# Which queue asks for a small on-chip copy: the doubling of the keys' high part, moved from ScalarE's queue to SP's

## The chip, the cores and the metric

The kernel runs on one core of a Trainium2 chip. A core has a matrix engine (PE, with its weight loads shown as PEld), a vector engine (VectorE, DVE in the profile), a scalar engine (ScalarE, ACT), a general engine (GpSimd, POOL) and SyncE (SP), which here only asks for transfers. The transfers themselves are carried out by 16 DMA engines; any engine's queue can ask for one, and two queues do in this kernel, SP's and ScalarE's. The metric is the device time of one execution in microseconds, the median of several runs.

## The reference

One layer of a hybrid decoder on 1024 tokens of width 1024, in float32:

```python
u = rms_norm(x, norm1_g)
aq, ak, av, hq, hf, hi, hg = jnp.split(u @ w_in, IN_SPLITS, axis=-1)
attn = rms_norm(dilated_attention(aq, ak, av), attn_norm_g)   # 8 heads of 64, three dilations
rec  = rms_norm(hgrn2_mixer(hq, hf, hi, lb), hgrn_norm_g) * silu(hg)   # 4 heads of 128
h = x + concatenate([attn, rec]) @ w_out
h = h + conv_glu(rms_norm(h, norm2_g), w_up, conv_w, conv_b, w_down)
out = rms_norm(h, final_norm_g)
```

The change lies in the attention heads. For each head, queries and keys (64 wide each) are projected from the normalised input, and each query's scores are the products with the keys before it, masked to the three dilated windows.

## The kernel before

**High and low parts.** Matrix products run on numbers that are split in two: a high part, rounded to PE's format (fp32r), and a low part, the rest. A product of two such numbers is the sum of high by high, high by low and low by high. For the scores the kernel saves a matmul with a trick of the partitions. A head is 64 wide and PE has 128 rows, so the tile `qs` holds the queries' high part in partitions 0 to 63 and their low part in partitions 64 to 127. The tile `kh` holds the keys' high part twice, in partitions 0 to 63 and again in 64 to 127: one matmul (L590) of `qs` and `kh` then gives high by high plus low by high. The second one (L591) adds the queries' high part by the keys' low part, from the tile `kl`.

**Who makes these tiles.** The function `qk_half(h, hf)` (L541) projects one head's queries and keys for one half of the tokens (512 of them), and its `evac` takes the result out of PSUM. VectorE multiplies it with the norm's factor into `x` (L550). ScalarE writes the queries' high part (L551) and the keys' high part into the upper partitions of `kh` (L552). The lower partitions are filled by another step: for heads 0 and 1 ScalarE copies from `x` once more (L554), for heads 2 to 7 a transfer copies the upper half of `kh` to its lower half (L556), 64 partitions of 512 numbers, 128 KB. VectorE then subtracts for the low parts (L557, L559). There are six heads and two halves, so L556 runs twelve times.

**The order of the work.** PE's instructions run in the order in which the code writes them (`manual_schedule` for PE alone). The instructions of the other engines and queues are ordered by the framework's planner, except where the code pins them (`keep_in_program_order`). During head h of the attention the code interleaves three kinds of work on PE: the scores of the next block of queries (`score_steps`), the transposes and value products of the present one (`value_steps`), and, as filler (`fill.run`), the projections that the next head needs. The list `beside` names that filler: `qk_block(h + 1)`, the two calls of `qk_half`, with pieces of the value projections around them. So `kh` of head h + 1 is made while head h is worked on, and the first half of its keys is read first by the scores of block 0, the second half from block 4 on.

**Scores and values.** `score_steps` multiplies, adds the mask and finds the row's extreme on VectorE (L595), takes the exponential on ScalarE (L599), and scales on POOL (L603). `value_steps` transposes the weights on PE (L618 to L625) into a PSUM tile `T` of two banks; ScalarE casts it to the high part (L628) and VectorE subtracts for the low part (L629), which also frees the bank; PE multiplies with the values (L637 to L641).

**The weights.** All weights come through the class `Ring` (L48). Its plan lists pieces of 128 by 512 numbers. For each, `fill` (L69) asks SP's queue for the load of the raw piece (L66; for the pieces of `want_iv` L253), lets ScalarE cast it to the high part (L86) and POOL or VectorE subtract for the low part (L88). There are five raw buffers and five finished pieces; `done` (L94) gives a finished piece back and calls `fill` again, so that in the code a new piece's load, cast and subtraction are written right there, inside the projection that used the old piece up. In this stage SP's queue asks for these loads alone; ahead of the stage it loads x and the mask (L391, L530), after it another mask (`hm`, L774) and later more. ScalarE's queue asks for the transfers of L556.

Of the kernel before, what the change touches and what calls it, by code (L numbers as in the profile page):

```python
# [43 lines left out]
def f32(ap):  # L44
    return ap.bitcast(F32)
# [157 lines left out]
def hybrid_kernel(ctx: ExitStack, tc: tile.TileContext, xT, w_qk, w_tok, w_hg, w_out, w_up,  # L203
                  w_down, vecs, amask, hmask, out):
    nc = tc.nc
# [245 lines left out]
    def dense(key, hf, evac, last, tag="mm"):  # L451

        t = halves[hf]
        ps = bank(tag, f"p{key}{hf}".translate({ord(x): "_" for x in "(', )"}))
        for c in range(NCT):
            hi, lo = ring.get((key, c // 4))
            s = slice((c % 4) * P, (c % 4 + 1) * P)
            b = between.get((key, hf, c), (0, 0))
            PE.matmul(ps, hi[:, s], uhi[:, c, t], start=(c == 0), stop=False)
            busy(b[0])  # L460
            PE.matmul(ps, hi[:, s], ulo[:, c, t], start=False, stop=False)
            PE.matmul(ps, lo[:, s], uhi[:, c, t], start=False, stop=(c == NCT - 1))
            busy(b[1])
            if last and c % 4 == 3:
                ring.done((key, c // 4))
            yield 0.65
        evac(ps)
# [60 lines left out]
    if True:  # L528
# [12 lines left out]
        def qk_half(h, hf, last, tag="mm"):  # L541
            t = halves[hf]

            def evac(ps):
                if hf == 0:
                    qk[h] = (at.tile([P, SEQ], F32R, tag="qs", name=f"qs{h}", bufs=NQ),
                             at.tile([P, SEQ], F32R, tag="kh", name=f"kh{h}", bufs=NQ), kls[h % NQ])
                qs, kh, kl = qk[h]
                x = at.tile([P, H2], F32, tag="x", name=f"x{h}_{hf}")
                DVE.tensor_mul(x, ps, R1[:, t])  # L550
                ACT.mul(qs[0:64, t], x[0:64], DH ** -0.5)  # L551
                ACT.copy(kh[64:128, t], x[64:128])  # L552
                if h < 2:
                    ACT.copy(kh[0:64, t], x[64:128])  # L554
                else:
                    nc.scalar.dma_start(f32(kh[0:64, t]), f32(kh[64:128, t]))  # L556
                DVE.scalar_tensor_tensor(qs[64:128, t], x[0:64], DH ** -0.5, f32(qs[0:64, t]),  # L557
                                         op0=ALU.mult, op1=ALU.subtract)
                DVE.tensor_sub(kl[0:64, t], x[64:128], f32(kh[64:128, t]))  # L559
            return dense(("qk", h), hf, evac, last, tag)  # L560
# [981 lines left out]
```

## Time and profile before

| | |
|---|---|
| median of 3 runs | 1203.69 us (1203.61 to 1204.4) |
| the profiled execution | 1204.6 us, of which 1202.6 us are the span of the trace |
| granted clock of PE | 0.997 |
| busy in the span | PE 99%, PEld 83%, DVE 79%, ACT 53%, POOL 25% |
| DMA queues | q1: 60528 packets, 101.41 MB; q10: 12176 packets, 21.44 MB |
| transfers of L556 | 12, of 128 KB each, on ScalarE's queue |
| first and last of them | 88.1 and 259.4 us from the span's start |

In the rows of the profile, a row of a group gives line, engine and operation, the tiles written and read, the count, and times; a row of the timeline gives the start and the length in microseconds, then the same, and in brackets the idle time of the engine before it with what ended it. "ACTq" and "SPq" are requests for transfers made by ScalarE's and SP's queues; they are not counted as busy time. "PE L590 MATMUL S<-kh,qs" is a score product that writes the tile S and reads `kh` and `qs`; buffer numbers are left out. In a table of stretches, each engine has its busy microseconds. Busy times of PE are partly modelled, since matmuls overlap.

### The profile page before, as it was taken

What the parts mean: (1) busy time and instruction counts of PE and PEld (TensorE: products, weight loads), DVE (VectorE), ACT (ScalarE), POOL (GpSimd) and SP (SyncE); (2) the same over time, 40 slices, a digit from 0 to 9 for tenths busy, and PEclk for the clock granted to TensorE, in tenths of its full rate; (3) what the DMA queues carried; (4) which work ended last, traced back from release to release, by engine and by line L of the source; (5) the groups of instructions that cost most, each with busy time, mean ns of one, the idle gap of its engine ahead of it and who ended that gap; (6) DMA issues with size and microseconds to landing.
All of it is one profiled execution on the core that took longest, in us unless ns stands there. A gap on an engine that the chain in (4) does not pass through costs nothing.

```text
span 1202.6 us, 17157 instructions
## 1 busy us (share of the span) xinstructions
PE 1186.7 (99%) x5854; PEld 994.9 (83%) x5854; DVE 948.9 (79%) x1776; ACT 631.5 (53%) x1219; POOL 297.9 (25%) x273
## 2 busy tenths in 40 slices
PE   9999999999999999999999999999999999999996
PEld 7988888888888888888888888888888888888886
DVE  7777776666878766485999889898888978957986
ACT  8766666667766564454543343333343444444553
POOL 1144446654001024413231222322223200000000
PEclk9999999999999999999999999999999999999998
DMA  7022222223101113432123322333223267434522
GB/s 271 13 75 62 63 62 92 80 72 115 41 31 62 61 56 115 141 129 80 44 70 114 110 83 97 123 114 120 82 97 115 96 213 251 153 101 159 169 101 89
DMA packets 72792, 123.94 MB, mean 103 GB/s; under 512 B 7552, under 2 KB 18048, under 8 KB 72704
## 3 DMA queue, kind: packets, MB, share of 16 engines
q1 hardware_dynamic: 60528, 101.41, 25.7%
q10 hardware_dynamic: 12176, 21.44, 4.9%
q8 instruction: 46, 0.75, 0.3%
q14 instruction: 42, 0.34, 0.1%
HBM read 97.65 MB, written 23.59 MB: 101 GB/s over the span
## 4 chain that ended last, share of the span: by engine, by line
PE 94%; DVE 2%; ACT 2%; issue 1%; DMA 0%; POOL 0%; SPq 0%; DVEq 0%; ACTq 0%; POOLq 0%
PE p L1143 11%; PE p L1142 11%; PE p L1141 11%; PE ds L1441 3%; PE ds L1440 3%; PE ds L1442 3%; PE po L1045 2%; PE po L1047 2%; PE po L1046 2%; PE da L1441 2%; PE da L1440 2%; PE da L1442 2%; PE S L590 1%; PE S L591 1%; PE O L637 1%; PE piv L513 1%
## 5 line engine op out<-in xcount | busy, mean ns | idle before, releaser
L88 POOL TENSOR_TENSOR wlo<-raww,whi 128x512 fp32r<-128x512 f32 x138 | 205.7, 1502 | 384.2 <-ACT whi L86 234.1
L86 ACT CAST whi<-raww 128x512 fp32r<-128x512 f32 x276 | 168.1, 617 | 191.5 <-DVE raww L120 68.6
L88 DVE TENSOR_TENSOR wlo<-raww,whi 128x512 fp32r<-128x512 f32 x139 | 99.3, 715 | 20.4 <-ACT whi L86 20.2
L86 ACT CAST whi<-r 128x512 fp32r<-128x512 f32 x70 | 43.6, 623 | 84.4 <-PE ds L1441 49.0
L603 POOL TENSOR_SCALAR P<-P,st 128x512 f32<-128x512 f32 (+2 forms) x96 | 58.0, 614 | 105.0 <-DVE st L600 90.7
L599 ACT ACTIVATE P<-P,st 128x128 f32<-128x128 f32 (+3 forms) x64 | 49.7, 777 | 26.9 <-DVE st L595 25.4
L88 DVE TENSOR_TENSOR wlo<-r,whi 128x512 fp32r<-128x512 f32 x70 | 47.9, 685 | 18.5 <-ACT whi L86 17.2
L1442 PE MATMUL ds<-fhi,wlo 128*128 128x512 f32 x160 | 62.3, 389 | 0.0
L1441 PE MATMUL ds<-flo,whi 128*128 128x512 f32 x160 | 62.3, 389 | 0.0
L1440 PE MATMUL ds<-fhi,whi 128*128 128x512 f32 x160 | 62.2, 389 | 0.0
L1141 PE MATMUL p<-b1h,whi 128*128 128x512 f32 x160 | 62.2, 389 | 0.0
L1142 PE MATMUL p<-b1l,whi 128*128 128x512 f32 x160 | 62.2, 389 | 0.0
L1143 PE MATMUL p<-b1h,wlo 128*128 128x512 f32 x160 | 62.2, 389 | 0.0
L629 DVE TENSOR_TENSOR t<-T,t 128x512 fp32r<-128x512 f32 (+1 forms) x80 | 50.7, 636 | 14.6 <-ACT t L628 13.3
L1163 DVE SCALAR_TENSOR_TENSOR cv<-g,vec,cv 128x511 f32<-128x511 f32 (+2 forms) x92 | 56.1, 614 | 4.7 <-ACT cv L1160 3.7
L628 ACT CAST t<-T 128x512 fp32r<-128x512 f32 (+1 forms) x80 | 43.1, 538 | 30.6 <-PE T L622 25.6
L1170 ACT ACTIVATE cv<-cv 128x512 f32<-128x512 f32 x44 | 27.8, 633 | 57.7 <-DVE cv L1163 57.7
L1414 POOL TENSOR_TENSOR facc<-facc,sqf 128x256 f32<-128x256 f32 x2 | 1.5, 738 | 223.4 <-ACT sqf L1413 223.4
L595 DVE CUSTOM_DVE_ANT_0 P<-S,mask 128x128 f32<-128x128 f32 (+3 forms) x64 | 35.5, 561 | 26.1 <-PE S L591 17.8
L88 DVE TENSOR_TENSOR flo<-rawf,fhi 128x512 fp32r<-128x512 f32 x70 | 47.8, 684 | 3.5 <-ACT fhi L86 3.5
L86 ACT CAST fhi<-rawf 128x512 fp32r<-128x512 f32 x70 | 43.1, 616 | 13.7 <-DMA rawf<-spT 6.6
L1440 PE MATMUL da<-fhi,whi 128*128 128x512 f32 x120 | 46.7, 389 | 0.0
(674 smaller groups left out, 3787.2 us busy)
## 6 DMA issues: line engine op xcount, KB each, us to landing
raww<-in_w_up_dram SPq DMA_DIRECT2D x88, 256.0 KB, 3.0
raww<-in_w_tok_dram SPq DMA_DIRECT2D x52, 256.0 KB, 2.7
rawf<-spT SPq DMA_DIRECT2D x40, 256.0 KB, 2.7
r<-in_w_down_dram SPq DMA_DIRECT2D x40, 256.0 KB, 3.2
raww<-in_w_hg_dram SPq DMA_DIRECT2D x32, 256.0 KB, 2.5
raww<-in_w_out_dram SPq DMA_DIRECT2D x32, 256.0 KB, 2.6
spB<-a ACTq DMA_DIRECT2D x30, 256.0 KB, 2.2
spT<-t ACTq DMA_DIRECT2D x30, 256.0 KB, 2.0
```

Source lines behind the costliest of these rows:

```text
L86: self.pin(self.high(hi[:, :w], raw))
L88: self.pin(low.tensor_sub(lo[:, :w], raw, f32(hi[:, :w])))
L599: ACT.activation(Pt[:, :n], Pt[:, :n], AF.Exp, bias=low, scale=-1.0, accum_out=st[:, 2:3])
L603: POOL.tensor_scalar(e, e, st[:, 3:4], 1.0, op0=ALU.mult, op1=ALU.mult)
L629: DVE.tensor_sub(t2[:, 1, :n], T[:, :n], f32(t2[:, 0, :n]))
L1141: PE.matmul(ps, hi[:, s], bhi, start=(start and n == 0), stop=False)
L1142: PE.matmul(ps, hi[:, s], blo, start=False, stop=False)
L1143: PE.matmul(ps, lo[:, s], bhi, start=False, stop=(stop and n == len(rhs) - 1))
L1163: DVE.scalar_tensor_tensor(dst, x, col(V_CW + j * NFF + f), dst, op0=ALU.mult, op1=ALU.add)
L1440: PE.matmul(ps[d], hi[:, s], ahi, start=(k == 0), stop=False)
L1441: PE.matmul(ps[d], hi[:, s], alo, start=False, stop=False)
L1442: PE.matmul(ps[d], lo[:, s], ahi, start=False, stop=(k == NPAIR - 1))
```

## The change

For heads 2 to 7, the transfer that copies the upper partitions of `kh` to its lower ones is asked for by SP's queue. What is copied, from where and to where, and who reads it are the same.

```diff
                 if h < 2:
                     ACT.copy(kh[0:64, t], x[64:128])
                 else:
-                    nc.scalar.dma_start(f32(kh[0:64, t]), f32(kh[64:128, t]))
+                    nc.sync.dma_start(f32(kh[0:64, t]), f32(kh[64:128, t]))
```

## The prediction

> **What bounds the kernel now.** I read the page first, then the stage in which the moved transfer runs (attention, 60 to 275 us of the span), then the waits of each engine there, and at last the engines instruction by instruction around single copies. The page's line for the matrix engine, the sum row of the busy time by stretches over 60 to 275 us (columns: length, then busy us of PE, of its weight loads, of DVE, ACT and POOL), and the only wait of PE in 84 to 275 us (total, times, longest):
>
> ```profile
> PE 1186.7 (99%) x5854; PEld 994.9 (83%) x5854; DVE 948.9 (79%) x1776; ACT 631.5 (53%) x1219; POOL 297.9 (25%) x273
> ```
>
> ```profile
> sum 215.00, PE 211.39 PEld 181.18 DVE 147.61 ACT 144.12 POOL 115.65; mean PE 30.20 PEld 25.88 DVE 21.09 ACT 20.59 POOL 16.52
> ```
>
> ```profile
> PE T L618 <- DVE t L629: 2.1, 4, 0.6
> ```
>
> PE carries the time: 211.39 of 215.00 us in this stage, against 144.12 of ScalarE (ACT). PE's order is written by hand, so a change elsewhere costs or gains only what it makes PE wait. All the waiting that PE shows from 84 to 275 us is 2.1 us, in four pieces. That is the most that this change can give back there by ending a wait that the profile names; what it can take is not bounded so.
>
> **What is removed: twelve requests from ScalarE's queue.** The rows of line 556, with the time from request to landing, and ScalarE's wait that names the copy ahead of it:
>
> ```profile
> L556 ACTq DMA_DIRECT2D kh<-kh x12: 467/468/522, 88.1 to 259.4; - x12
> ...
> DMA to landing us min/median/max: 2.2/2.3/4.2
> ```
>
> ```profile
> ACT t L628 <- ACT kh L552: 2.7, 5, 0.5
> ```
>
> Twelve requests of 0.468 us are 5.6 us of ScalarE's queue. Two requests come per head, one for each half of the tokens, and the two behave differently. The first half of head 2, then its second half:
>
> ```profile
> 87.50 0.62 ACT L552 CAST kh<-x 64x512 fp32r<-64x512 f32 x1
> 88.14 0.94 ACT L599 ACTIVATE P<-P,st 128x768 f32<-128x768 f32 x1
> 88.14 0.52 ACTq L556 DMA_DIRECT2D kh<-kh  x1
> ...
> 89.57 0.62 ACT L86 CAST whi<-raww 128x512 fp32r<-128x512 f32 x1
> ```
>
> ```profile
> 98.81 0.47 ACTq L556 DMA_DIRECT2D kh<-kh  x1
> 99.33 0.59 ACT L628 CAST t<-T 128x512 fp32r<-128x512 f32 x1 [0.54 <-ACT kh L552]
> ```
>
> In the first half the request (88.14, 0.52) runs while the exponential ahead of it (88.14, 0.94) keeps ScalarE busy: its removal gives nothing. In the second half ScalarE stands still for it: the next cast (L628) begins at 99.33, 0.54 us after the copy of L552, with the request in between. The wait row counts five such gaps, 2.7 us. So what the change gives to ScalarE's compute is 2.7 us, not 5.6, and the question is whether PE sees any of it. After the gap of head 2, on VectorE (DVE) and on PE:
>
> ```profile
> 99.76 0.69 DVE L559 TENSOR_TENSOR kl<-x,kh 64x512 fp32r<-64x512 f32 x1
> 100.48 0.29 DVE L595 CUSTOM_DVE_ANT_0 P<-S,mask 128x128 f32<-128x128 f32 x1
> ...
> 100.69 0.42 DVE L595 CUSTOM_DVE_ANT_0 P<-S,mask 128x256 f32<-128x256 f32 x1
> ...
> 101.04 0.69 DVE L629 TENSOR_TENSOR t<-T,t 128x512 fp32r<-128x512 f32 x1
> ```
>
> ```profile
> 101.78 0.33 PE L618 MATMUL T<-ident,P 128*128 128x128 f32 x1 [0.50 <-DVE t L629]
> ```
>
> PE loses 0.50 us until VectorE's subtraction (L629, 101.04 + 0.69 = 101.73) frees a PSUM bank. That subtraction reads what ScalarE cast at 99.33, which was there at 99.92; it began at 101.04 because VectorE first did L559 and two of L595, back to back. With the gap gone the cast ends at 99.38, and VectorE still comes to L629 at 101.04. So the 0.54 us end in VectorE's queue: I cost the gain at nothing. The cover is 101.04 - 99.92 = 1.12 us of VectorE's earlier work; were it gone, up to 0.50 us at each of the four waits, 2.1 us in all, would come back.
>
> The Trainium skill's page "DMA: Bandwidth & Descriptors" (section "Issuing engines are not separate DMA queues") says that asking from several engines saves no more than the sequencer's own time for the request, and that this is usually small. The trace agrees on the size (0.468 us) and goes further: of the twelve times only five show as a gap, and none of these five reaches PE. By the rule alone the move would be worth at most 5.6 us of ScalarE; by the rows the sum is zero.
>
> **What is added: twelve requests in SP's queue, and a wait on ScalarE.** SP has so far asked for weights in this stage. The requests around head 2, and the POOL subtraction that gives one of their buffers free:
>
> ```profile
> 67.77 0.33 SPq L66 DMA_DIRECT2D raww<-in_w_tok_dram  x1
> ```
>
> ```profile
> 91.96 0.33 SPq L66 DMA_DIRECT2D raww<-in_w_tok_dram  x1
> ```
>
> ```profile
> 99.21 0.33 SPq L66 DMA_DIRECT2D raww<-in_w_tok_dram  x1
> ```
>
> ```profile
> 97.90 1.28 POOL L88 TENSOR_TENSOR wlo<-raww,whi 128x512 fp32r<-128x512 f32 x1
> ```
>
> A request takes SP 0.33 us and the queue is idle for microseconds between them. The signal from another engine is cheap: POOL ended at 99.18 and SP asked at 99.21. So in the first half the copy would still be asked for within 0.1 us of 88.14, with 3.8 us to the next load: nothing is queued behind it that could go. In the second half the copy (98.81) and a load (99.21) fall close together. If the copy stands first, it ends at 98.81 + 0.33 = 99.14, before the load can start. If the load stands first, the copy is asked for at 99.54, 0.73 us late, and lands by the nearest rows between 99.54 + 2.3 = 101.8 and, if its bytes stand behind the load's, 99.21 + 2.7 + 2.3 = 104.2 (a load's 2.7 us is in the row below). Who waits for it is the score product of the first block of queries that needs the second half of the keys:
>
> ```profile
> 113.12 0.30 PE L590 MATMUL S<-kh,qs 128*128 128x320 f32 x1
> ```
>
> ```profile
> raww<-in_w_tok_dram SPq DMA_DIRECT2D x52, 256.0 KB, 2.7
> ```
>
> That is 9 us after the worse landing: cost zero either way. The load at 99.21 is five pieces ahead of use (five raw buffers), so a delay of 0.4 us is not felt. Sum: 0 removed from the path, 0 added to it. The profiled execution took 1204.6 us (span 1202.6), 0.9 above the median of the runs, so the sum made against it carries over to the median as it is: **1203.7 us**.
>
> **The rivals.** A change of 0.2%, 2.4 us, is about what a measurement of this kernel can tell from no change.
>
> *Faster: the gap on ScalarE is what PE waits for.* Were VectorE to take L629 ahead of the two of L595, all four waits of PE could go: 1203.7 - 2.1 = 1201.6, or at most 1201.0 if the five gaps count whole (2.7). For it: the waits come right behind the second-half copies. Against it: the cast had ended 1.12 us before VectorE began L629. It decides where L629 becomes the first in VectorE's queue. Chance 0.08, of which 0.03 passes 0.2%.
>
> *Slower: the weight loads stand behind the copy.* In the code the ring (L69 to L97) writes a load only once an older piece is given back, and the piece cast at 89.57 is written after the first-half copy of head 2. Its load was asked for at 67.77: the loads come in order, that of 91.96 is the fifth behind the piece cast at 89.57, whose buffer it takes. If SP's queue kept the code's order, that load would wait for the copy: 88.14 + 0.33 = 88.5, landing at 91.2, and ScalarE's in-order cast of 89.57 would come 1.6 us late. ScalarE's next idle pieces are these:
>
> ```profile
> 91.27 0.59 ACT L628 CAST t<-T 128x512 fp32r<-128x512 f32 x1 [0.68 <-PE T L622]
> 92.17 1.05 ACT L599 ACTIVATE P<-P,st 128x896 f32<-128x896 f32 x1 [0.31 <-DVE st L595]
> ...
> 94.49 0.59 ACT L628 CAST t<-T 128x512 fp32r<-128x512 f32 x1 [1.19 <-PE T L622]
> ```
>
> They take up 0.7 us soon and 2.2 us within five, so PE loses between 0 and 1.6 us a head; at 0.8 for six heads it is 4.9 us, **1208.6 us**, at most 1213.5. The point from which it decides: a load asked for after 89.57 - 2.7 = 86.9. Against it speaks the end of the stage, where SP also asks for a mask:
>
> ```profile
> 275.85 20.56 SPq L66 DMA_DIRECT2D raww<-in_w_hg_dram  x10
> 296.46 0.42 SPq L774 DMA_DIRECT2D hm<-in_hmask_dram  x1
> ```
>
> In the code only five of these loads can be written before L774 (the ring holds five); ten were asked for before it. So the planner that orders SP's queue lets requests whose buffers are free pass one that must wait, and a load free at 67.77 would not be put behind a copy of 88.14. Chance 0.08.
>
> *Slower: the copy stands behind a load.* The least slack is in heads 6 and 7, first half. Head 6, then head 7: the copy's request, the load that follows it, and the first score product.
>
> ```profile
> 215.91 0.47 ACTq L556 DMA_DIRECT2D kh<-kh  x1
> ```
>
> ```profile
> 219.02 0.34 SPq L66 DMA_DIRECT2D raww<-in_w_qk_dram  x1
> ```
>
> ```profile
> 220.63 0.22 PE L590 MATMUL S<-kh,qs 128*128 128x128 f32 x1
> ```
>
> ```profile
> 250.17 0.47 ACTq L556 DMA_DIRECT2D kh<-kh  x1
> ```
>
> ```profile
> 253.51 0.37 SPq L253 DMA_DIRECT2D raww<-in_w_tok_dram  x1
> ```
>
> ```profile
> 255.13 0.22 PE L590 MATMUL S<-kh,qs 128*128 128x128 f32 x1
> ```
>
> Landing 2.2 us later, the copies leave 2.5 and 2.8 us. Put behind the loads they would be asked for at 219.36 and 253.88 and land at 221.6 and 256.1, 0.9 and 1.0 us late, or, if their bytes follow the load's (2.7 + 2.2), 3.3 us late each: 1.9 to 6.6 us, in the middle 4.2, **1207.9 us**. Against it: these loads become free only through a cast that ScalarE does after the copy's source is ready, so a planner that goes by readiness puts the copy first, with 3 us to spare. Chance 0.06. The Trainium skill's page "DMA: Bandwidth & Descriptors" (section "Queues, rings and completion order") says that each DMA engine takes one queue's work in order and alternates between queues by packets, so a copy on SP's queue follows the loads asked for before it instead of sharing with them; by that the upper price, 6.6 us, would hold. No row of this trace can show it: no copy goes through SP's queue yet.
>
> *The order elsewhere changes.* All engines but PE are ordered by the planner, which now has other queues to fill; single instructions on VectorE or ScalarE may swap places. Bounded by the 2.1 us of waits on the gain side, taken as the same on the other: 1201.6 to 1205.8. Chance 0.06, of either sign.
>
> That the change does nothing at all to ScalarE (the 0.54 us gap remains, for another reason) would give the forecast's time too, and stands within it.
>
> **How the numbers follow.** No change to be seen: 0.72. Faster by the gap: 0.08. Loads behind the copy: 0.08. Copy behind a load: 0.06. Other order: 0.06. The range reaches down to the whole gain, 1201.0, and up to 1206.5, which takes in the low end of the copy behind a load (1205.6); left out are the loads behind the copy but for their mildest form (0.07), the dearer part of the late copy (0.05) and tails of the rest (0.03). Faster by over 0.2%: 0.03 from the gap, 0.02 from order and the forecast's tail, together 0.05. Slower by over 0.2%: 0.07 + 0.05 + 0.03 = 0.15. Within: 0.80.
>
> **What would show it.** Right: twelve requests of L556 on SP, those of the first halves within 0.2 us of ScalarE's copy; ScalarE's wait for L552 gone (2.7 us less idle) and its cast some 0.5 us earlier; VectorE's L629 and PE's four waits of 0.5 us where they were; the loads of line 66 and 253 no later than before by more than a microsecond; PE's busy sum in the stage within 1 us. Wrong: PE waiting for ScalarE's L86 or L628, or the score product of L590 waiting for the transfer, or a new order on VectorE in which L629 precedes L595.

## The result, and the profile after

| | before | changed |
|---|---|---|
| median of 22 runs | 1204.38 us | 1206.05 us |
| lowest to highest | 1203.61 to 1205.59 | 1205.08 to 1207.08 |
| profiled execution | 1204.6 us, span 1202.6 | 1206.33 us, span 1204.5 |

The ratio is 1.0014 with a 95% interval of 1.0008 to 1.0020. The changed kernel is slower by 1.7 us, a seventh of a per cent: less than the bound that the prediction set for a visible change, but more than nothing. The time is inside the predicted range; the predicted sum, zero, is not what happened. Over these 22 runs the kernel before stands at 1204.38 us, 0.7 above the three runs that the prediction started from.

The views that the prediction read, now of the changed kernel: the page's line of PE, the sum over 60 to 275 us, the rows of line 556, and all that PE waits for in 84 to 280 us (total, times, longest).

```profile
PE 1187.9 (99%) x5854; PEld 995.2 (83%) x5854; DVE 951.7 (79%) x1776; ACT 631.7 (52%) x1219; POOL 296.0 (25%) x273
```

```profile
sum 215.00, PE 209.97 PEld 179.74 DVE 147.06 ACT 141.96 POOL 113.46; mean PE 30.00 PEld 25.68 DVE 21.01 ACT 20.28 POOL 16.21
```

```profile
L556 SPq DMA_DIRECT2D kh<-kh x12: 467/467/529, 88.1 to 261.6; - x12
...
DMA to landing us min/median/max: 2.2/2.3/3.7
```

```profile
PE S L590 <- DVE st L595: 2.1, 4, 0.6
PE T L618 <- DVE t L629: 1.4, 4, 0.4
```

The twelve requests are on SP and land as quickly as before (median 2.3 us). ScalarE's wait behind L552, 2.7 us before, is gone from its list. And yet PE has done 1.4 us less work by 275 us (209.97 against 211.39). A new wait has come: four times PE's score product (L590) waits for VectorE's mask-and-extreme step (L595), 2.1 us in all. The old four waits for L629 are still there, a little shorter (1.4 us for 2.1).

Where the time is lost can be read from the requests themselves, since they come at one place in each head. First one row of the kernel before (head 3), then the first-half requests of heads 2 to 6 in the changed kernel:

```profile
118.04 0.47 ACTq L556 DMA_DIRECT2D kh<-kh  x1
```

```profile
88.11 0.53 SPq L556 DMA_DIRECT2D kh<-kh  x1
...
118.55 0.47 SPq L556 DMA_DIRECT2D kh<-kh  x1
...
149.09 0.47 SPq L556 DMA_DIRECT2D kh<-kh  x1
...
179.59 0.47 SPq L556 DMA_DIRECT2D kh<-kh  x1
...
218.11 0.47 SPq L556 DMA_DIRECT2D kh<-kh  x1
```

Head 2's request comes at the old time (88.11 for 88.14), head 3's 0.5 us late, head 6's 2.2 us late (218.11 for 215.91): about 0.55 us are lost in each of the four heads that lie between, and none before. That makes 2.2 us in this stage. The last store of the execution lands 0.3 us sooner than before (2.3 us after its request, 2.6 before), so the spans differ by 1.9 us. One of the four heads tells the story. VectorE in the work of head 1, right after the first-half copy for head 2, before and then changed:

```profile
90.06 0.67 DVE L595 CUSTOM_DVE_ANT_0 P<-S,mask 128x512 f32<-128x512 f32 x1
90.66 0.08 DVE L595 DVE_READ_ACCUMULATOR2_ANT st<- 128x1 f32 x1
90.66 0.54 DVE L629 TENSOR_TENSOR t<-T,t 128x384 fp32r<-128x384 f32 x1
91.13 0.41 DVE L647 TENSOR_TENSOR ot<-O,ot 64x256 f32<-64x256 f32 x1
```

```profile
89.67 0.56 DVE L629 TENSOR_TENSOR t<-T,t 128x384 fp32r<-128x384 f32 x1
90.15 0.41 DVE L648 TENSOR_TENSOR raw<-O,ot 64x256 f32<-64x256 f32 x1
90.59 0.42 DVE L647 TENSOR_TENSOR ot<-O,ot 64x256 f32<-64x256 f32 x1
90.93 0.67 DVE L595 CUSTOM_DVE_ANT_0 P<-S,mask 128x512 f32<-128x512 f32 x1
```

The order is another one. VectorE used to take the scores of block 6 (L595) at 90.06 and the subtraction L629 after it; now L629 and an addition of an older block (L647) go first, and L595 starts at 90.93, 0.87 us later. It frees one of the two score banks. On PE, before and then changed:

```profile
90.96 0.27 PE L622 MATMUL T<-ident,P 128*128 128x128 f32 x1
90.99 0.48 PE L590 MATMUL S<-kh,qs 128*128 128x512 f32 x1
```

```profile
90.92 0.27 PE L622 MATMUL T<-ident,P 128*128 128x128 f32 x1
91.66 0.50 PE L590 MATMUL S<-kh,qs 128*128 128x512 f32 x1 [0.47 <-DVE st L595]
```

The next score product needs that bank and starts 0.70 us later, counted from the common point (the changed trace runs 0.03 us ahead here). The profile names only 0.47 us of it, since it counts idle time from the modelled end of the matmul before (90.92 + 0.27 = 91.19); in the kernel before, the score product began 0.03 us after the start of that matmul, well before its modelled end. A second swap follows: ScalarE takes the exponential of block 7 before a cast (L628), and VectorE that cast's subtraction only after L550. At the end of the head the old wait for L629 is 0.2 us shorter, which leaves 0.5 us a head.

Set side by side, the orders of the two kernels differ in no instruction of PE and POOL. On VectorE and ScalarE the two swaps appear in heads 1 to 4; beyond that VectorE has one addition (L648) moved in heads 4 to 6, and ScalarE has lost its twelve requests. The loads on SP are in the same order, with the copies between them.

### The profile page after: what moved, and what is told of

Same layout as the page of the kernel before. It is cut to its first block, busy times and chain, and to the rows that moved or that the text cites. A ratio compares the mean times of both kernels' runs of the same rounds, so it can differ in the third digit from the quotient of the medians.

```text
span 1204.5 us, 17198 instructions
## 1 busy us (share of the span) xinstructions
PE 1187.9 (99%) x5854; PEld 995.2 (83%) x5854; DVE 951.7 (79%) x1776; ACT 631.7 (52%) x1219; POOL 296.0 (25%) x273
## 4 chain that ended last, share of the span: by engine, by line
PE 93%; DVE 3%; ACT 2%; issue 1%; DMA 0%; POOL 0%; SPq 0%; DVEq 0%; ACTq 0%; POOLq 0%
PE p L1142 11%; PE p L1143 11%; PE p L1141 11%; PE ds L1440 3%; PE ds L1442 3%; PE ds L1441 3%; PE po L1045 2%; PE po L1047 2%; PE po L1046 2%; PE da L1440 2%; PE da L1441 2%; PE da L1442 2%; PE O L637 1%; PE S L590 1%; PE piv L513 1%; PE piv L515 1%
## 5 line engine op out<-in xcount | busy, mean ns | idle before, releaser
L599 ACT ACTIVATE P<-P,st 128x128 f32<-128x128 f32 (+3 forms) x64 | 49.7, 776 | 34.7 <-DVE st L595 29.1
L629 DVE TENSOR_TENSOR t<-T,t 128x512 fp32r<-128x512 f32 (+1 forms) x80 | 50.6, 635 | 12.5 <-ACT t L628 11.5
L628 ACT CAST t<-T 128x512 fp32r<-128x512 f32 (+1 forms) x80 | 43.0, 538 | 24.9 <-PE T L622 22.3
L595 DVE CUSTOM_DVE_ANT_0 P<-S,mask 128x128 f32<-128x128 f32 (+3 forms) x64 | 35.4, 561 | 26.0 <-PE S L591 19.6
```

Source lines behind the costliest of these rows:

```text
L599: ACT.activation(Pt[:, :n], Pt[:, :n], AF.Exp, bias=low, scale=-1.0, accum_out=st[:, 2:3])
L629: DVE.tensor_sub(t2[:, 1, :n], T[:, :n], f32(t2[:, 0, :n]))
```

## The experiments

The theory from this comparison, called the order theory: the copy costs nothing on SP's queue, and the loss is the planner's other order on VectorE. The rivals: the queue theory (the copies, the loads behind them or the signal to SP come late) and the gap theory, the prediction's own "faster" rival (ScalarE's gap of 0.54 us is what PE's four old waits came from).

In the edits, `behind(later, earlier)` holds one instruction behind another of the same engine; it sets the order of issue and adds no wait. The names stand for: `lo` and `hi` the subtraction L629 and the cast L628 of (head, block pair, part), `red` the mask-and-extreme step L595 and `exp` the exponential L599 of (head, block), `x` the projection's multiplication L550, `ot` and `raw` the additions L647 and L648. The added lines shift the line numbers of these kernels by 7 (in one by 13).

**1. SP's queue with the old order.**

```diff
-                    nc.scalar.dma_start(f32(kh[0:64, t]), f32(kh[64:128, t]))
+                    nc.sync.dma_start(f32(kh[0:64, t]), f32(kh[64:128, t]))
+        for h in range(NH):
+            if 1 <= h <= 4:
+                behind(("lo", h, 1, 1), ("red", h, 6, 0))
+                behind(("raw", h, 0), ("red", h, 6, 512))
+            if 4 <= h <= 6:
+                behind(("raw", h, 2), ("lo", h, 3, 2))
```

Holding the first swap back undoes the second too: every engine then has the order of the kernel before, and only the queue of the twelve copies differs.

> The copies stay on SP's queue, and VectorE, ScalarE and POOL are held to the instruction order of the kernel before. The order theory (the planner, no longer counting the request on ScalarE, let one of VectorE's subtractions pass a mask-and-extreme of the scores, and PE waits for a score bank): the 1.7 us are gone, 1204.4 +- 0.4 us, and PE's four waits of 0.5 us for L595 with them. The queue theory (the copy or the loads on SP's queue come late, or the signal to SP costs): it stays at 1206.0. The gap theory of the first rival in the prediction: below the kernel before, 1202.3, since ScalarE's gaps of 0.54 us are gone and the order is the old one.

Measured: 1203.93 us against 1204.09 of the kernel before, ratio 0.9998 (0.9990 to 1.0007). The loss is gone. The queue alone costs nothing, and with it the gaps on ScalarE are gone too, to no gain. PE's waits for L629 (here L636) stay. The second row, one wait of 0.4 us, is no news: it stands at 280 us in all these traces, in the kernel before at 280.15, just behind the stretch.

```profile
PE T L625 <- DVE t L636: 2.3, 4, 0.6
PE S L597 <- DVE st L602: 0.4, 1, 0.4
```

**2. ScalarE's queue with the new order.** The reverse: nothing is moved, but both swaps are forced.

```diff
+            if 1 <= h <= 4:
+                behind(("red", h, 6, 0), ("ot", h, 0))
+                behind(("red", h, 6, 0), ("lo", h, 1, 1))
+                behind(("red", h, 6, 512), ("raw", h, 0))
+                behind(("raw", h - 1, 3), ("lo", h, 1, 1))
+                behind(("hi", h, 2, 1), ("exp", h, 7))
+                behind(("lo", h, 2, 1), ("x", h + 1, 1))
+            if 4 <= h <= 6:
+                behind(("lo", h, 3, 2), ("raw", h, 2))
```

> The copies stay on ScalarE's queue as in the kernel before, and VectorE and ScalarE are held to the instruction order of the changed kernel. The order theory: as slow as the changed kernel although nothing is moved, 1206.0 +- 0.5 us, with four waits of PE of 0.5 us for L595; a little more if the requests now also delay ScalarE. The queue theory: as the kernel before, 1204.4.

Measured: 1206.51 us against 1204.09, ratio 1.0016 (1.0008 to 1.0025): the whole loss without the change. PE's waits are those of the changed kernel:

```profile
PE S L597 <- DVE st L602: 2.1, 4, 0.6
PE T L625 <- DVE t L636: 1.4, 4, 0.4
```

**3 and 4. Half of the copies moved**, nothing held.

```diff
+                    (nc.scalar if hf else nc.sync).dma_start(...)   # 3: first half on SP
+                    (nc.sync if hf else nc.scalar).dma_start(...)   # 4: second half on SP
```

> Only the copies of the first half of the tokens go through SP's queue, those of the second half stay on ScalarE's. Nothing is pinned. The order theory: it is the request of the first half that stood ahead of the cast which the swapped subtraction needs, so the whole loss is here: 1206.0 +- 0.4 us. The queue theory: the loss belongs to the requests that fall together with a load, which are those of the second half: 1204.4; or, spread over all twelve, about 1205.2.

> Only the copies of the second half of the tokens go through SP's queue. The order theory: VectorE's order around the swap is the old one, so 1204.4 +- 0.4 us, though ScalarE's gaps of 0.54 us are all gone and each copy is asked for close to a load. The queue theory: 1206.0, or 1205.2 if the loss is spread. The gap theory: 1202.3.

Measured: with the first half on SP 1205.95 us, ratio 1.0013 (1.0005 to 1.0022), and both swaps are there; with the second half on SP 1203.46 us, ratio 0.9994 (0.9985 to 1.0003), and neither is. So the loss comes with the six requests of the first half, those that ran beside the exponential and kept ScalarE from nothing, and not with the six that left the gaps. The queue theory falls with runs 1 to 4, the gap theory with 1 and 4.

**5 and 6. One swap at a time**, copies on ScalarE's queue.

```diff
+                behind(("hi", h, 2, 1), ("exp", h, 7))              # 5: the later swap alone
+                behind(("lo", h, 2, 1), ("x", h + 1, 1))
```

```diff
+                behind(("red", h, 6, 0), ("ot", h, 0))              # 6: the earlier swap alone,
+                behind(("red", h, 6, 0), ("lo", h, 1, 1))           #    the later one held back
+                behind(("red", h, 6, 512), ("raw", h, 0))
+                behind(("raw", h - 1, 3), ("lo", h, 1, 1))
+                behind(("exp", h, 7), ("hi", h, 2, 1))
+                behind(("x", h + 1, 1), ("lo", h, 2, 1))
```

> Copies on ScalarE's queue; of the two swaps between the orders only the later one is made: ScalarE takes the exponential of block 7 ahead of a cast, and VectorE the new projection ahead of that cast's subtraction. The order theory puts the loss on the earlier swap, in which PE waits for a score bank: no change, 1204.2 +- 0.5 us. If the later swap carries the loss: 1206.

> Copies on ScalarE's queue; only the earlier swap is made: VectorE does the subtraction L629 of block 1 ahead of the scores L595 of block 6 in heads 1 to 4. The order theory: the whole loss, four waits of PE of 0.5 us for L595, less what the later waits for L629 give back, 1205.9 +- 0.5 us. If the later swap carries the loss: 1204.2.

Measured: the later swap alone 1203.60 us, ratio 0.9997 (0.9988 to 1.0005); the earlier alone 1207.29 us, ratio 1.0027 (1.0017 to 1.0036). The place was right, the size was not: with the earlier swap the kernel is 3.2 us slower, more than expected, and the later swap gives part of it back. In the traces PE loses 2.9 us in the attention heads with the earlier swap alone and 2.2 us in the changed kernel, which has both. Both traces of this pair also have a wait in the up projection that comes without these swaps too (see 9 to 12), so the medians are no exact price of them. In the run with the later swap alone, the planner also put one cast and its subtraction a step earlier in head 4. PE's waits with the earlier one alone, then with the later one alone:

```profile
PE S L597 <- DVE st L602: 2.1, 4, 0.6
PE T L625 <- DVE t L636: 2.0, 4, 0.5
```

```profile
PE T L625 <- DVE t L636: 1.5, 4, 0.4
PE S L597 <- DVE st L602: 0.4, 1, 0.4
```

The later swap shortens the waits for L629 by about 0.6 us (2.0 to 1.4 beside the earlier one, 2.1 to 1.5 without it). The earlier one adds four waits of 2.1 us in all, and each stop costs PE more than its named wait: 0.71 to 0.87 us in this trace, where 0.47 to 0.59 are named.

**7. VectorE's order at the old waits.** The kernel before, with the point that the prediction's faster rival names as deciding.

```diff
+            if 1 <= h <= 4:
+                behind(("red", h + 1, 0, 0), ("lo", h, 3, 0))
```

> The kernel before, copies on ScalarE's queue with its gaps, but VectorE is made to take L629 ahead of the two of L595 at the start of the next head, in heads 1 to 4. This is the point that the prediction's first rival names. The order theory: PE's four waits of 0.5 us for L629 go, 1204.2 - 2.1 = 1202.1 us. If those waits came from ScalarE's gap behind the request, they stay, at 1204.2, since the gap is still there; and if the later L595 makes PE wait in their place, 1204 or more.

Measured: 1201.97 us against 1204.08, ratio 0.9981 (0.9973 to 0.9990), just the 2.1 us of the four waits. (The planner moved a few instructions behind this point too, such as the next cast and some additions; the run shows the four points with what follows from them.) The gap on ScalarE is still there, and PE waits for it no more. ScalarE, VectorE and PE of head 2 in this kernel:

```profile
98.94 0.59 ACT L635 CAST t<-T 128x512 fp32r<-128x512 f32 x1 [0.54 <-ACT kh L559]
```

```profile
99.38 0.69 DVE L566 TENSOR_TENSOR kl<-x,kh 64x512 fp32r<-64x512 f32 x1
100.09 0.69 DVE L636 TENSOR_TENSOR t<-T,t 128x512 fp32r<-128x512 f32 x1
100.70 0.28 DVE L602 CUSTOM_DVE_ANT_0 P<-S,mask 128x128 f32<-128x128 f32 x1
```

```profile
100.84 0.33 PE L625 MATMUL T<-ident,P 128*128 128x128 f32 x1
```

The cast comes after its gap as before and ends at 99.53; VectorE is busy until 100.07 and takes the subtraction at 100.09; the transpose starts with no wait.

**8. The copy forced behind a load.** As experiment 1, with the first-half copy of each head behind the load that follows it in SP's queue, the prediction's third rival.

```diff
+                    seen["copy", h, hf] = nc.sync.dma_start(f32(kh[0:64, t]), f32(kh[64:128, t]))
...
+        for h, n in zip(range(2, NH), (22, 28, 34, 40, 50, 60)):   # loads: the requests for weights, in order
+            tc.add_manual_dep(seen["copy", h, 0].ins, loads[n - 4].ins.name, ...)   # order alone, as in behind
```

> The copies on SP's queue with the old order on the other engines, and in all six heads the copy of the first half is put behind the load that follows it. This is the prediction's third rival, forced. By its price: heads 6 and 7 make PE wait 0.9 to 3.3 us each for the doubled keys, so 1204.0 + 1.9 to 6.6 = 1205.9 to 1210.6 us; heads 2 to 5 land in time or just so (4 us of slack are used up of 6.5). If the slack is larger than the rows said, or the queue theory had the cost elsewhere: 1204.0.

Measured: 1208.28 us against 1204.08, ratio 1.0033 (1.0020 to 1.0045). The price was foreseen as 1.9 to 6.6, in the middle 4.2, and it is 4.2. That it meets the middle is chance: the two copies landed 3.0 and 2.7 us after their requests instead of 2.2, which gives waits of 3.1 us by name, and PE lost 3.6 us at them in the trace. The two waits are in heads 6 and 7, and there are none in heads 2 to 5:

```profile
PE S L603 <- DMA kh<-kh: 3.1, 2, 1.7
```

```profile
219.41 0.34 SPq L66 DMA_DIRECT2D raww<-in_w_qk_dram  x1
219.80 0.47 SPq L569 DMA_DIRECT2D kh<-kh  x1
```

```profile
222.89 0.33 PE L603 MATMUL S<-kh,qs 128*128 128x128 f32 x1 [1.71 <-DMA kh<-kh]
```

So the slack that the prediction read off for heads 6 and 7 (2.5 and 2.8 us) is real, and the planner's choice of the copy before the load is what keeps it.

**9 to 12. Both together.** The lead of L629 from experiment 7 with the copies on SP, in three forms: all copies on SP with the order of experiment 1 held (the "seventh run" of the texts below); only the second half's copies on SP and nothing else held, run twice; all on SP without holding the addition L648.

```diff
+            if 1 <= h <= 4:
+                behind(("red", h + 1, 0, 0), ("lo", h, 3, 0))
```

> All copies on SP's queue, the old order on the other engines, and VectorE's L629 ahead of the two of L595 at the next head's start. Both parts that the runs showed, at once. The order theory: as with the copies on ScalarE, 1202.0 +- 0.4 us, faster than both kernels, since the queue itself costs nothing. If ScalarE's gaps cost something once the waits behind them are gone: up to 0.5 us a head less, 1200 us.

> Only the second half's copies on SP's queue, nothing pinned but VectorE's L629 ahead of the two of L595 at the next head's start. The order theory: the planner keeps the old order by itself at the earlier swap, so as the run before in this pair, 1202.0 +- 0.4 us. A loss against it would say that the mixed queues cost something.

> As the seventh run (all copies on SP, old order at the earlier swap, L629 ahead of the two of L595), but without holding a late addition (L648) of heads 4 to 6 behind a subtraction. VectorE, ScalarE and POOL then have the order of the run with half the copies on SP, so only the queue of the first half's copies differs from that. The order theory: 1202.0 +- 0.4 us, and the 1.1 us of the seventh run came from the held addition or from a wait of a later stage (0.7 us at 580 us in its trace). If asking SP for the first half's copies itself costs: 1203.0.

> The run with the second half's copies on SP and L629 ahead once more, on the same chip as the run beside it: 1202.0 +- 0.4 us by every theory; it says how far two visits of one kernel lie apart.

Measured: all on SP 1203.03 us, ratio 0.9988 (0.9979 to 0.9997); half on SP 1201.95, ratio 0.9983 (0.9975 to 0.9992), and again 1202.23, ratio 0.9984 (0.9975 to 0.9993); all on SP with L648 free 1202.88, ratio 0.9988 (0.9979 to 0.9997). All are faster than both kernels; with half the copies on SP the median is that of experiment 7, with all of them on SP it is 0.7 to 1.1 us higher, which the order theory did not foresee. The held addition is not the reason (1202.88 without it). The traces show three things beside PE's listed waits.

First, the attention heads gain less than in experiment 7: 1.1 to 1.3 us from 84 to 300 us in these four, 2.2 there. The planner's order differs once more. In experiment 7, then in the run with half the copies on SP, ScalarE in head 2:

```profile
99.87 0.58 ACT L635 CAST t<-T 128x512 fp32r<-128x512 f32 x1 [0.34 <-PE T L629]
```

```profile
100.84 0.40 ACT L606 ACTIVATE P<-P,st 128x128 f32<-128x128 f32 x1 [2.01 <-DVE st L602]
...
101.24 0.57 ACT L635 CAST t<-T 128x512 fp32r<-128x512 f32 x1
```

With no gap on ScalarE the next cast now stands behind an exponential that has to wait; VectorE's next subtraction comes later, and PE stops once more in each of three heads, with 0.1 us of idle time shown and 0.25 to 0.35 us lost.

Second, both kernels with all copies on SP show a wait that the half-moved one has nowhere. It stands at 609 us, in the up projection, far behind the last copy:

```profile
PE p L1158 <- DVE wlo L88: 0.7, 1, 0.7
```

It was also there in experiments 5 (0.6 us) and 6 (0.7), with the copies on ScalarE's queue, so it does not belong to SP's copies as such. In just these four traces one VectorE instruction ahead of it is long. With half the copies on SP, then with all of them:

```profile
584.03 0.68 DVE L1216 TENSOR_TENSOR t<-uf,uf 128x512 f32<-128x512 f32 x1
```

```profile
584.19 1.78 DVE L1221 TENSOR_TENSOR t<-uf,uf 128x512 f32<-128x512 f32 x1
```

VectorE is 1.1 us late from there on, and PE meets it at 609 us. What makes the instruction long stays open, and so does whether it is long in every execution of these kernels: one execution of each was traced.

Third, the last store of the execution lands 2.6 to 3.0 us after its request where all copies are on ScalarE's queue, 2.3 where all are on SP's (2.6 in experiment 8), and 2.0 where half are:

```profile
out_dram<-h SPq DMA_DIRECT2D x1, 128.0 KB, 2.6
```

```profile
out_dram<-h SPq DMA_DIRECT2D x1, 128.0 KB, 2.0
```

The first is the kernel before, the second the run with half the copies on SP. Why is open as well. With such terms at the end, differences of half a microsecond between two of these medians say nothing about the attention heads.

## Why the prediction was right in range and wrong in its sum

**What bounds the kernel** held: PE, through its waits alone. What the runs gain and lose in the attention heads they gain and lose at stops of PE.

**The gain costed at nothing** held. The five gaps on ScalarE went and PE's time in the attention heads did not move (experiments 1 and 4: by 0.2 us and by nothing). The reason given was the right one, VectorE's queue: experiment 7 made L629 the first in it, left the gap in place, and got the 2.1 us. The bound of the faster rival, 1201.6 us, and its deciding point were right; only the change itself does not bring it about.

**The requests on SP costed at nothing** held. In the second half the load stood first, as one of the two cases said: in the changed trace SP asks for the load at 99.72 and for the copy at 100.10, and the copy lands at 103.2, well before it is read. The Trainium skill's page "DMA: Bandwidth & Descriptors" (section "Queues, rings and completion order") has each DMA engine take up a queue's work in order. The prediction let its upper price of 6.6 us, the copy's whole time behind the load's, follow from that. Experiment 8 shows less: the load asked for at 219.41 and the copy at 219.80 both took 3.0 us, so the copy landed 0.4 us after the load and not a whole transfer later. The two overlapped, and the price was 4.2.

**The rival with the loads behind the copy** did not occur. The loads come in the same order as before, and the load that follows head 2's first copy is asked for at 91.90 (91.96 before), so none was held behind it.

**The step that failed** is the sentence "In the first half the request (88.14, 0.52) runs while the exponential ahead of it (88.14, 0.94) keeps ScalarE busy: its removal gives nothing." For ScalarE that is true. The sum, though, took every other engine to keep its order, and it did not: with the request on ScalarE's queue the planner had put L629 behind L595 on VectorE, and without it the two are the other way round (experiments 3 and 4 show that these six requests decide it). The prediction carried this only as "The order elsewhere changes", with 2.1 us either way and a chance of 0.06. The 1.7 us lie within its bound (1201.6 to 1205.8 from a median of 1203.7, that is up to 2.1), but that is luck in part: the bound on the side of the loss was "taken as the same on the other", from no row, and with the earlier swap alone (experiment 6) the loss was 3.2 us. The upper end of the whole range, 1206.5, had been set with the late copy in mind. No instruction was named. It could have been: L629 of block 1 needs the cast that stood right behind the request in ScalarE's queue, and it stood in VectorE's queue next to an L595 that frees a score bank. Why the planner swaps them is an inference: its account of ScalarE's time has the cast ready earlier by the length of a request. No run looks into that account.

**What was to be seen:** twelve requests on SP and the gaps gone, as said; L629 and PE's waits "where they were", not so; PE's busy sum moved by 1.4 us where less than 1 was said, and the loads came up to 2.2 us later where a microsecond was said. "a new order on VectorE in which L629 precedes L595" was listed as a sign of a wrong forecast, and it came, at another pair of the two than the one meant.

## What to carry to other kernels

Where a planner orders the engines, a moved instruction is an edit to every queue that shares work with it: compare the orders of both kernels before reading the moved instruction's own cost, and hold the old order to measure the move by itself. Here the move cost nothing, the side effect 1.7 us. And a gap on an engine that is not the bottleneck says little; look for the instruction that frees what the bottleneck waits for, and ask what stands ahead of it in its queue: putting that one forward was worth 2.1 us in the kernel before.

## What was not expected of the hardware

A short stop of PE can cost more than its named wait: 0.71 to 0.87 us at the score products of experiment 6, where 0.47 to 0.59 us are named. The name counts from the modelled end of the matmul before, and the stop also takes away the overlap of the two. At the waits for L629 the difference is small: taking away 0.50 us of named wait gave PE 0.56 us (experiment 7).

The six copies of the second half of the tokens, which SP asks for 0.4 to 0.8 us behind a load in the changed kernel, took 2.4 to 3.7 us to land, the first halves 2.2 or 2.3. The load takes 2.7 us itself, so they did not wait for the whole of it. Nor is it the shared queue that makes them slow: on ScalarE's queue, in the kernel before, the second halves took 2.3 to 4.2 us.

And the same VectorE instruction on the same shapes, a TENSOR_TENSOR of 128x512, took 0.68 us in one build and 1.78 us in another. Each of these traces has 36 to 38 VectorE instructions that are 0.9 to 1.2 us longer than the median of their form, nearly all at the same places; no run here shows what lengthens them.
